# Seven of sixteen row blocks by a seven-product scheme, and one weight sum formed by transfers

## The chip, the cores and the metric

The kernel runs on one core of a Trainium2 chip. The metric is the device time of one execution in microseconds (us); the time before is the median of three runs. A profile holds one execution. Its engines are PE (the matrix engine), DVE (the vector engine), ACT (the scalar engine), POOL (the general-purpose engine) and SP, which here only issues transfers. ACT and POOL can issue transfers too; each engine issues its own in order.

## The reference

Four layers work on 256 frames of 1024 channels. Each adds a token mixer (retention, convolution, stick-breaking attention, retention) and then a feed-forward part:

```python
def squared_relu_mlp(xn, w1, w2):
    h = jax.nn.relu(xn @ w1)
    return (h * h) @ w2

for i in range(DEPTH):                      # 4
    ...
    x = x + m
    x = x + squared_relu_mlp(rms_norm(x, norm_ffn[i]), ffn_w1[i], ffn_w2[i])
return rms_norm(x, final_norm)
```

All data is float32; `w1` is 1024x4096 and `w2` is 4096x1024. The change concerns `(h * h) @ w2`, in the text the *down product*: 256 rows by 4096 by 1024, once per layer.

## The kernel before

**Split operands.** A float32 product is made of three matmuls on rounded operands: each operand is a high part (a cast, `wh` for a weight) plus a low part (source minus high part, `wl`), and high·high, high·low and low·high are added. Casts of weights are done by ACT (L362), the subtractions by DVE (L369), a tile of 128x1024 at a time. There are 5 buffers for `wh` and 5 for `wl`, so ACT's cast of a new tile waits until PE has read the last matmul of the tile five back.

**Weights.** They come from `in_w` in chunks of 1 MB (`raw`, 3 buffers) by SP in a fixed order (L348). A chunk holds two tiles of 128x1024.

**The down product** (`down`, L684). The 4096 rows of `w2` are 16 units `kb` of 256 rows; one unit is one 1 MB chunk. `C[t, c]` are four 128x512 accumulators in PSUM (`acc`) for two row halves t and two column halves c. `triple` (matmul at L689) issues the three matmuls of one product and keeps them in program order, so that PE runs the units in the order of the table `MIXED` and then `REST`.

A *plain* unit takes 8 products, thus 24 matmuls, two casts and two subtractions of 1024 columns. A *fast* unit (`FAST`) views its weights as four 128x512 blocks b11, b21, b12, b22 and the activations as four blocks of 128x128 columns, and takes 7 products by Strassen's scheme in Winograd's form, thus 21 matmuls. It needs the weight sums t1 = b11+b12, t3 = b12+b22, t2 = t1+b22 and t4 = t2+b21, added on DVE in `fast_unit` at L385, cast at L392 and subtracted at L393 in pieces of 512 columns. Its activation sums (`s1` to `s4`) are formed when the unit's activations leave the first product (L644 to L653) and rest in `big` or `z` tiles until used. Four of the seven products go to accumulators of their own in PSUM (`mis`: p1, p5, p7, p6), shared by all fast units; the others go straight to `C`.

After `MIXED` the four are combined into `C` through `big` tiles on ACT and DVE (L728 to L735, L759, L760), while PE goes on with the units of `REST`: first column half 0 of all of them, then column half 1, with one load of each chunk. When a column half is done the results are scaled, added to the residual, and handed to the next layer's mixer (L774, L787). The last layer ends in the final norm.

**Order.** Within an engine, instructions stand in an order that a scheduler sets at build time from estimated durations, unless `keep_in_program_order` binds them; at run time every engine runs its own list in order and waits for semaphores. Of temporary 128x512 tiles (`t`) there are 10. Constants, the retention decays among them, sit in one tile `cst`.

## Time and profile before

| what | value |
|---|---|
| median of three runs | 1329.37 us (1328.36 to 1329.39) |
| the profiled execution's own time | 1329.23 us |
| its span on the core | 1327.5 us |
| PE busy | 1316.6 us (99%), 7703 matmuls |
| DVE busy | 1063.9 us (80%) |
| ACT busy | 860.1 us (65%) |
| POOL busy | 154.1 us (12%) |
| `MIXED` of the first layer in the trace | 293.56 to about 356 us |

The span runs from the first to the last instruction of the profiled execution; the run's time is 1.7 us longer. "Busy" counts instructions in execution. On PE each matmul is drawn longer than its distance to the next, since they overlap. In a timeline a row gives start, duration, engine, line, operation, output and inputs, and in brackets how long the engine sat idle before it and what released it.

### The profile page before, as it was taken

The page shows a single profiled execution, that of the slowest core. Times are in us where ns is not written, and L with a number is a line of the kernel's source. Part 1 is how long each engine was busy: PE and PEld are TensorE (multiplying, and loading weights), DVE is VectorE, ACT ScalarE, POOL GpSimd, SP SyncE. Part 2 cuts the span into 40 slices and gives each one's busy share as a digit, 9 for nine tenths or more (in the row PEclk, how much of TensorE's full clock was granted, in tenths as well). Part 3 has the DMA queues.
Part 4 walks back from the last instruction along what each step waited for, and adds up shares of the span by engine and source line. Part 5 has one row for each costly group of instructions (what it writes and reads, how often), then busy time and mean ns, then how long its engine had stood idle before and what let it go on. Part 6 is the DMA issues. An engine that isn't in the chain of part 4 may idle for free.

```text
span 1327.5 us, 20237 instructions
## 1 busy us (share of the span) xinstructions
PE 1316.6 (99%) x7703; PEld 1133.6 (85%) x7703; DVE 1063.9 (80%) x1805; ACT 860.1 (65%) x1407; POOL 154.1 (12%) x169
## 2 busy tenths in 40 slices
PE   9999999999999999999999999999999999999998
PEld 8988888888899898888888898888888888888886
DVE  7987877779778688798788588798798776798985
ACT  7555546886566478766668678866675555567663
POOL 3554411000009110000000010000020000100000
PEclk9999999999999999999999999999999999999999
DMA  8666655545765655545453355555454554555552
GB/s 312 211 218 223 227 206 191 190 159 201 277 240 152 202 182 193 188 161 220 158 189 130 127 193 189 190 190 210 169 193 171 189 180 160 206 202 191 177 192 94
DMA packets 46049, 253.95 MB, mean 191 GB/s; under 512 B 5376, under 2 KB 10112, under 8 KB 18560
## 3 DMA queue, kind: packets, MB, share of 16 engines
q1 hardware_dynamic: 43360, 245.32, 52.4%
q0 software_dynamic: 1728, 4.72, 0.9%
q10 hardware_dynamic: 864, 2.62, 0.6%
q8 instruction: 60, 0.98, 0.3%
q14 instruction: 37, 0.30, 0.1%
HBM read 245.99 MB, written 6.65 MB: 190 GB/s over the span
## 4 chain that ended last, share of the span: by engine, by line
PE 96%; DVE 2%; ACT 1%; DMA 0%; issue 0%
PE acc L577 22%; PE acc L689 19%; PE acc L573 11%; PE acc L1107 6%; PE acc L1109 6%; PE acc L1108 6%; PE mis L689 3%; PE acc L557 3%; PE acc L558 3%; PE acc L559 3%; PE mis L577 2%; PE acc L1275 1%; PE mis L573 1%; PE acc L1408 1%; DVE wl L393 1%; DVE t L385 1%
## 5 line engine op out<-in xcount | busy, mean ns | idle before, releaser
L369 DVE TENSOR_TENSOR wl<-raw,wh 128x1024 fp32r<-128x1024 f32 (+1 forms) x420 | 512.5, 1231 | 122.1 <-ACT wh L362 119.1
L362 ACT CAST wh<-raw 128x1024 fp32r<-128x1024 f32 (+1 forms) x420 | 433.2, 1041 | 232.4 <-PE acc L689 68.6
L577 PE MATMUL acc<-z,wh 128*128 128x512 f32 x1152 | 399.4, 393 | 0.0
L573 PE MATMUL acc<-z,wl 128*128 128x256 f32 x1152 | 317.6, 280 | 0.0
L689 PE MATMUL acc<-wh,big 128*128 128x512 f32 x800 | 255.9, 391 | 0.0
L577 PEld LDWEIGHTS acc<-z,wh 128*128 128x128 f32 x1152 | 214.2, 187 | 47.1
L573 PEld LDWEIGHTS acc<-z,wl 128*128 128x128 f32 x1152 | 216.9, 189 | 2.4 <-DVE t L602 0.3
L689 PEld LDWEIGHTS acc<-wh,big 128*128 128x128 f32 x800 | 150.2, 188 | 30.7
L689 PE MATMUL acc<-wl,big 128*128 128x512 f32 x400 | 156.2, 390 | 0.5 <-DVE wl L369 0.5
L1107 PE MATMUL acc<-wh,z 128*128 128x512 f32 x352 | 138.6, 394 | 0.0
L1109 PE MATMUL acc<-wh,z 128*128 128x512 f32 x352 | 137.3, 390 | 0.0
L1108 PE MATMUL acc<-wl,z 128*128 128x512 f32 x352 | 137.2, 390 | 0.0
L601 ACT COPY t<-acc 128x256 f32<-128x256 f32 x154 | 53.1, 371 | 57.3 <-PE acc L577 55.4
L689 PEld LDWEIGHTS acc<-wl,big 128*128 128x128 f32 x400 | 75.1, 188 | 17.6 <-DVE wl L369 1.8
L1107 PEld LDWEIGHTS acc<-wh,z 128*128 128x128 f32 x352 | 66.1, 188 | 15.2 <-issue 2.2
L1109 PEld LDWEIGHTS acc<-wh,z 128*128 128x128 f32 x352 | 66.1, 188 | 14.8 <-issue 0.8
L1108 PEld LDWEIGHTS acc<-wl,z 128*128 128x128 f32 x352 | 66.1, 188 | 13.3
L602 DVE TENSOR_TENSOR t<-acc,t 128x256 f32<-128x256 f32 x154 | 59.7, 419 | 17.9 <-ACT t L601 16.0
L392 ACT CAST wh<-t 128x512 fp32r<-128x512 f32 x80 | 47.1, 619 | 35.2 <-DVE t L385 12.3
L557 PE MATMUL acc<-z,wh 128*128 128x256 f32 x224 | 63.7, 284 | 0.0
L492 POOL TENSOR_TENSOR t<-t,t 128x512 f32<-128x512 f32 x15 | 24.2, 1612 | 339.1 <-ACT t L487 308.7
L558 PE MATMUL acc<-z,wh 128*128 128x256 f32 x224 | 63.4, 283 | 0.0
(300 smaller groups left out, 2098.6 us busy)
## 6 DMA issues: line engine op xcount, KB each, us to landing
raw<-in_w SPq DMA_DIRECT2D x214, 1024.0 KB, 4.9
strip<-st POOLq DMA_DIRECT2D x36, 128.0 KB, 4.0
big<-strip SPq DMA_DIRECT2D x18, 256.0 KB, 5.9
big<-in_gn SPq DMA_DIRECT2D x16, 256.0 KB, 5.3
raw<-in_w SPq DMA_DIRECT2D x7, 512.0 KB, 7.4
raw<-hd SPq DMA_DIRECT2D x8, 263.0 KB, 5.2
raw<-hd SPq DMA_DIRECT2D x8, 131.5 KB, 3.6
wh<-in_w ACTq DMA_DIRECT2D x2, 512.0 KB, 6.3
```

What stands on the lines that cost most here:

```text
L362: nc.scalar.copy(hi[:, s], src[:, s])
L369: self.nc.vector.tensor_sub(lo[:, s], src[:, s], hi[:, s])
L557: nc.tensor.matmul(o, wh[:, kk, cs], ah, start=st, stop=False, **kw)
L558: nc.tensor.matmul(o, wh[:, kk, cs], al, start=False, stop=False, **kw)
L573: mm = nc.tensor.matmul(ps[m][:, :S], wl[:, kk, cs], a[:, :S], start=first and kk == 0, stop=False, **kw)
L577: nc.tensor.matmul(ps[m], wh[:, kk, cs], a, start=False, stop=last and kk == 3, **kw)
L601: nc.scalar.copy(o[:, s], ps[m][:, S:])
L602: nc.vector.tensor_add(o[:, s], ps[m][:, :S], o[:, s])
L689: mm = nc.tensor.matmul(o, l, r, start=start and n == 0, stop=stop and n == 2, skip_group_check=True)
L1107: nc.tensor.matmul(ps[t], zh[:, s], wh[:, kk], start=k == 0, stop=False, skip_group_check=True)
L1108: nc.tensor.matmul(ps[t], zh[:, s], wl[:, kk], start=False, stop=False, skip_group_check=True)
L1109: nc.tensor.matmul(ps[t], zl[:, s], wh[:, kk], start=False, stop=k == 7, skip_group_check=True)
```

## The change

It changes the down product and where some constants and activation sums are kept.

- `FAST` grows from five units to seven: 9 and 12 are added. `MIXED` begins with two plain units (0, 1) in place of one, has the fast units 9, 12 and 13, 14 next to each other, and ends with fast unit 15. `REST` shrinks from four units to three (8, 10, 11).
- The weight sum t3 = b12+b22 is no longer added on DVE. `sum_ahead` loads b12 into a `t` tile by SP and then adds b22 to it with an accumulating transfer that POOL issues (line numbers of the changed kernel: L385 and L386). Two are issued before the first unit, then one in each fast unit, two fast units ahead. The POOL ones keep their program order.
- t1 = b11+b12 is written over b12 in the `raw` tile (L415), so that t1 and b22 stand side by side and are cast (L399) and subtracted (L400) as one piece of 1024 columns. t3 and t2 share one weight tile, t4 has half of another. t2 and t4 are still DVE adds (L417, L419).
- `issue_after` places a fast unit's first cast, and its first add, behind an earlier subtraction in the build-time order.
- The activation sums of seven fast units need more room than those of five: `spare` takes `big` tiles for the first two fast units, a tile shared with the retention decays (tag "decay") for unit 9, and `z0` to `z7` for the rest. The decays therefore have a tile of their own and are loaded a second time for the last layer (4 transfers of 192 KB). The final norm's gain, which sat in `z6` and `z7`, is now loaded into `big` tiles after `MIXED`.

```diff
@@ -56,9 +56,9 @@
-FAST = (5, 6, 13, 14, 15)
-MIXED = (0, 5, 1, 2, 6, 3, 13, 4, 14, 7, 15, 8)
-REST = (9, 10, 11, 12)
+FAST = (5, 6, 9, 12, 13, 14, 15)
+MIXED = (0, 1, 5, 2, 6, 3, 9, 12, 4, 13, 14, 7, 15)
+REST = (8, 10, 11)
 OUT_ORDER = [(kb, p) for g in (0, 2) for kb in range(4) for p in (g, g + 1)]
@@ -108,6 +108,7 @@
 NUNIT = len(PLAN)
 UPC = 2
 NCHUNK = NUNIT // UPC
+DECAY = [PLAN.index(u) // UPC + n for u in (PLAN[DST * UPC], ("ret_w_in", 1, "b", 0, DK)) for n in range(RH)]
@@ -348,10 +349,14 @@
                     nc.sync.dma_start(self.rawt[:, a : a + h], self.w_d[n][:, a : a + h])
             for _ in range(min(2, len(self.later))):
                 self.later.pop(0)()
-            i = self.un // UPC - DST
-            if 0 <= i < RH:
-                n = CCOL["D"] + i * 384
-                self.tc.keep_in_program_order(nc.sync.dma_start(self.cst[:, n : n + 384], self.cst_d[:, n : n + 384]))
+            if self.un // UPC in DECAY:
+                i = DECAY.index(self.un // UPC) % RH
+                if i == 0:
+                    self.decay = self.cp.tile([P, RH * 384], F32, name=self.nm("decay"), tag="decay")
+                n = i * 384
+                self.tc.keep_in_program_order(
+                    nc.sync.dma_start(self.decay[:, n : n + 384], self.cst_d[:, CCOL["D"] + n : CCOL["D"] + n + 384])
+                )
         o = self.un % UPC
         src = self.rawt[:, o * 1024 : (o + 1) * 1024]
@@ -366,32 +371,54 @@
     def unit_lo(self, u):
         hi, lo, src, cuts = u
         for s in cuts:
-            self.nc.vector.tensor_sub(lo[:, s], src[:, s], hi[:, s])
+            self.lo_ins = self.nc.vector.tensor_sub(lo[:, s], src[:, s], hi[:, s]).ins
         return hi, lo
+    def sum_ahead(self, l):
+        nc = self.nc
+        m = len(self.ahead)
+        if m < len(FAST):
+            kb = [k for k in MIXED if k in FAST][m]
+            d = self.w_d[PLAN.index(("ffn_w2", l, "a", kb, 0)) // UPC]
+            t = self.tmp()
+            nc.sync.dma_start(t, d[:, 1024:1536])
+            self.tc.keep_in_program_order(nc.gpsimd.dma_start(t, d[:, 1536:2048], accum_op=ALU.add))
+            self.ahead[kb] = t
+
+
     def fast_unit(self, name, l, kb):
         nc = self.nc
-        ah, al = self.unit((name, l, "a", kb, 0))
+        out = []
+
+        def parts(*ts):
+            h, g = (self.wp.tile([P, 1024], F32R, name=self.nm(t), tag=t) for t in ("wh", "wl"))
+            a = 0
+            for t in ts:
+                c = slice(a, a + t.shape[1])
+                nc.scalar.copy(h[:, c], t)
+                self.lo_ins = nc.vector.tensor_sub(g[:, c], t, h[:, c]).ins
+                a = c.stop
+            out.extend((h[:, c : c + 512], g[:, c : c + 512]) for c in range(0, a, 512))
+
+        with self.tc.issue_after(self.lo_ins):
+            hi, lo = self.unit((name, l, "a", kb, 0))
+        out = [(hi[:, c : c + 512], lo[:, c : c + 512]) for c in (0, 512)]
         o = self.un % UPC * 1024
         assert PLAN[self.un] == (name, l, "a", kb, 512) and o
         self.un += 1
-        b11, b21, b12, b22 = (self.rawt[:, n * 512 : (n + 1) * 512] for n in range(4))
-        t1, t2, t3, t4 = (self.tmp() for _ in range(4))
-        out = [(ah[:, :512], al[:, :512]), (ah[:, 512:], al[:, 512:])]
-        h = None
-        for n, (dst, x, y) in enumerate(((None, b22, None), (t1, b11, b12), (t3, b12, b22), (t2, t1, b22), (t4, t2, b21))):
-            if dst is not None:
-                nc.vector.tensor_add(dst, x, y)
-            else:
-                dst = x
-            if n % 2 == 0:
-                h = self.wp.tile([P, 1024], F32R, name=self.nm("wh"), tag="wh")
-                g = self.wp.tile([P, 1024], F32R, name=self.nm("wl"), tag="wl")
-            c = slice(n % 2 * 512, (n % 2 + 1) * 512)
-            nc.scalar.copy(h[:, c], dst)
-            nc.vector.tensor_sub(g[:, c], dst, h[:, c])
-            out.append((h[:, c], g[:, c]))
+        b11, b21, t1, b22 = (self.rawt[:, i * 512 : (i + 1) * 512] for i in range(4))
+        t3 = self.ahead[kb]
+        self.sum_ahead(l)
+        t2, t4 = (self.tmp() for _ in range(2))
+        with self.tc.issue_after(self.lo_ins):
+            nc.vector.tensor_add(t1, b11, t1)
+        parts(self.rawt[:, 1024:2048])
+        nc.vector.tensor_add(t2, t1, b22)
+        parts(t3, t2)
+        nc.vector.tensor_add(t4, t2, b21)
+        parts(t4)
+        out[2], out[3] = out[3], out[2]
         return out
@@ -623,7 +650,16 @@
     def ffn(self, i, nxt):
         nc = self.nc
         last = nxt is None
-        h, rb, fast = [], [], {}
+        h, rb, fast, room = [], [], {}, []
+
+        def spare(n):
+            if n < 4:
+                return self.bigt(F32R)
+            if n < 6:
+                if n == 4:
+                    room.append(self.cp.tile([P, RH * 384], F32R, name=self.nm("room"), tag="decay"))
+                return room[0][:, (n - 4) * 512 : (n - 3) * 512]
+            return self.zp.tile([P, 512], F32R, name=self.nm("z"), tag=f"z{n - 6}")
         def act(ps):
@@ -644,11 +680,7 @@
                 nc.vector.tensor_sub(v3(x[:, :S], 2, P), v3(s[:, :S], 2, P), v3(s, 2, S)[:, :, P:])
                 nc.vector.tensor_sub(s2, s[:, :P], s1)
                 nc.vector.tensor_sub(s4, s[:, S : S + P], s2)
-                n = 2 * FAST.index(p) - 4
-                hi, lo = (
-                    self.bigt(F32R) if n < 0 else self.zp.tile([P, 512], F32R, name=self.nm("z"), tag=f"z{n + o}")
-                    for o in range(2)
-                )
+                hi, lo = (spare(2 * FAST.index(p) + o) for o in range(2))
                 nc.scalar.copy(hi, x)
                 nc.vector.tensor_sub(lo, x, hi)
@@ -698,6 +730,9 @@
             return [tuple(v3(x, 2, 512)[:, kk] for x in w) for kk in range(2)]
         C = {}
+        self.ahead = {}
+        for _ in range(2):
+            self.sum_ahead(i)
         for kb in MIXED:
             if kb not in FAST:
                 for c in range(2):
@@ -734,6 +769,7 @@
         nc.vector.tensor_add(uq, u, e5)
         nc.vector.tensor_add(C[1, 1], C[1, 1], uq)
+        hook(C, "gain")
         if i == 0:
             self.strip_t = []
...
@@ -844,6 +878,10 @@
                 ))
         def hook(C, at):
+            if at == "gain":
+                for c in range(2):
+                    gain.append(self.bigt())
+                    nc.sync.dma_start(gain[c], self.fin_d[:, c * 512 : (c + 1) * 512])
             if at:
                 return
```

In the changed kernel the plain subtraction is at L374, the cast at L367 and the load of a chunk at L349. Over the program PE issues 6756 rows where it issued 6780, DVE 1822 for 1782, ACT 1364 for 1352, SP 314 for 282 and POOL 202 for 174. Three places of the first layer follow.

**DVE inside `MIXED`.** Before, a fast unit (13, its chunk is `raw_3625`), with the two subtractions of the plain unit 3 (`raw_3591`) in between:

```order
L385 TENSOR_TENSOR t_771_3631<-raw_3625 128x512
L385 TENSOR_TENSOR t_773_3633<-raw_3625 128x512
L385 TENSOR_TENSOR t_772_3632<-t_771_3631,raw_3625 128x512
L385 TENSOR_TENSOR t_774_3634<-t_772_3632,raw_3625 128x512
L369 TENSOR_TENSOR wl_3594<-raw_3591,wh_3593 128x1024
L369 TENSOR_TENSOR wl_3610<-raw_3591,wh_3609 128x1024
L369 TENSOR_TENSOR wl_3628<-raw_3625,wh_3627 128x1024
L393 TENSOR_TENSOR wl_3636<-raw_3625,wh_3635 128x512
L393 TENSOR_TENSOR wl_3636<-t_771_3631,wh_3635 128x512
L393 TENSOR_TENSOR wl_3644<-t_773_3633,wh_3643 128x512
L393 TENSOR_TENSOR wl_3644<-t_772_3632,wh_3643 128x512
```

After, the fast unit 9 (`raw_3558`, its t3 is `t_721`) and the begin of unit 12:

```order
L374 TENSOR_TENSOR wl_3561<-raw_3558,wh_3560 128x1024
L415 TENSOR_TENSOR raw_3558<-raw_3558 128x512
L417 TENSOR_TENSOR t_760_3567<-raw_3558 128x512
L419 TENSOR_TENSOR t_761_3568<-t_760_3567,raw_3558 128x512
L400 TENSOR_TENSOR wl_3571<-raw_3558,wh_3570 128x1024
L400 TENSOR_TENSOR wl_3576<-t_721_3394,wh_3575 128x512
L400 TENSOR_TENSOR wl_3576<-t_760_3567,wh_3575 128x512
L400 TENSOR_TENSOR wl_3583<-t_761_3568,wh_3582 128x512
L374 TENSOR_TENSOR wl_3610<-raw_3607,wh_3609 128x1024
L415 TENSOR_TENSOR raw_3607<-raw_3607 128x512
L417 TENSOR_TENSOR t_772_3616<-raw_3607 128x512
L419 TENSOR_TENSOR t_773_3617<-t_772_3616,raw_3607 128x512
```

One add of 512 columns is gone; the two subtractions of [t1] and [b22] have become one of 1024; unit 12's follow with no plain unit between.

**SP at the head of the stage.** Before (L348 is the load of a chunk):

```order
L348 DMA raw_3387<-in_w 128x2048
L348 DMA raw_3421<-in_w 128x2048
L348 DMA raw_3455<-in_w 128x2048
L348 DMA raw_3506<-in_w 128x2048
L348 DMA raw_3540<-in_w 128x2048
L348 DMA raw_3591<-in_w 128x2048
```

After (L349 is the load of a chunk; L385 is here the load of b12 into a `t` tile, not the add that had this number before). `raw_3441` is unit 2, `raw_3475` the fast unit 6, `t_702` the sum of the first fast unit 5:

```order
L349 DMA raw_3441<-in_w 128x2048
L349 DMA raw_3475<-in_w 128x2048
L385 DMA t_702_3310<-in_w 128x512
L385 DMA t_703_3313<-in_w 128x512
L385 DMA t_721_3394<-in_w 128x512
L385 DMA t_742_3481<-in_w 128x512
L349 DMA raw_3524<-in_w 128x2048
L349 DMA raw_3558<-in_w 128x2048
L385 DMA t_759_3564<-in_w 128x512
L349 DMA raw_3607<-in_w 128x2048
L349 DMA raw_3656<-in_w 128x2048
L385 DMA t_771_3613<-in_w 128x512
```

Four loads for sums now stand between the chunk of unit 6 and the next one; the POOL transfers that add b22 to them (L386) follow each of them in time.

**ACT at the first fast unit.** Before (unit 5, `t_708` is t1, `t_709` t3, `t_710` t2, `t_711` t4; then unit 1):

```order
L412 CAST big_3274<-t_688_3272 128x256
L412 CAST big_3277<-t_688_3272 128x256
L392 CAST wh_3342<-t_708_3338 128x512
L392 CAST wh_3350<-t_710_3340 128x512
L392 CAST wh_3350<-t_709_3339 128x512
L652 CAST z_3284<-t_691_3280 128x512
L392 CAST wh_3358<-t_711_3341 128x512
L362 CAST wh_3389<-raw_3387 128x1024
L362 CAST wh_3405<-raw_3387 128x1024
```

After (unit 5 is `raw_3388`, `t_722` is t2 and `t_702` the transferred t3; `raw_3441` is unit 2):

```order
L439 CAST big_3290<-t_694_3288 128x256
L439 CAST big_3293<-t_694_3288 128x256
L399 CAST wh_3400<-raw_3388 128x1024
L399 CAST wh_3405<-t_722_3397 128x512
L399 CAST wh_3405<-t_702_3310 128x512
L399 CAST wh_3412<-t_723_3398 128x512
L684 CAST z_3300<-t_697_3296 128x512
L367 CAST wh_3443<-raw_3441 128x1024
L367 CAST wh_3459<-raw_3441 128x1024
```

The cast of the transferred t3 stands third of unit 5's four; the cast of t4, one activation cast and all of unit 2 stand behind it.

More of the change, by code (lines that the diff above doesn't have):

```diff
@@ L268, in __init__ @@
         self.prm = self.cp.tile([P, NPCOL - NP0], F32, name="prm", tag="prm")
-        self.cst = self.cp.tile([P, NCCOL], F32, name="cst", tag="cst")
+        self.cst = self.cp.tile([P, CCOL["D"]], F32, name="cst", tag="cst")
         self.first = [self.raw.tile([P, RAWW], F32, name=f"raw{n}", tag="raw") for n in range(3)]
@@ L831, in final @@
         self.table("sqrt_and_others")
-        gain = [self.zp.tile([P, 512], F32, name=self.nm("gain"), tag=f"z{6 + c}") for c in range(2)]
-        for c in range(2):
-            nc.sync.dma_start(gain[c], self.fin_d[:, c * 512 : (c + 1) * 512])
+        gain = []
         rows = []
@@ L1005, in retention @@
                     out=a[t], in0=ps[:, c0:c1], scalar=ck[:, t * 4 + h : t * 4 + h + 1],
-                    in1=self.c("D", c1 - c0, h * 384 + c0), op0=ALU.mult, op1=ALU.mult,
+                    in1=self.decay[:, h * 384 + c0 : h * 384 + c1], op0=ALU.mult, op1=ALU.mult,
                 )
```

## The prediction

> **What bounds the kernel now.** I read the page first: span, busy shares, granted clock, the chain that ended last.
>
> ```profile
> span 1327.5 us, 20237 instructions
> PE 1316.6 (99%) x7703; PEld 1133.6 (85%) x7703; DVE 1063.9 (80%) x1805; ACT 860.1 (65%) x1407; POOL 154.1 (12%) x169
> PEclk9999999999999999999999999999999999999999
> PE 96%; DVE 2%; ACT 1%; DMA 0%; issue 0%
> ```
>
> PE is busy all through, its clock is full in all slices, and the chain is PE for 96%. So time is won by giving PE fewer matmuls, as long as DVE (80%) and ACT keep ahead of it. Second the chain in order of time, in the first layer's down product (start, length, what):
>
> ```profile
> 303.34 1.15 DVE wl L369
> 304.53 10.96 PE acc L689 x47
> ...
> 319.57 6.12 PE acc L689 x27
> ```
>
> 27 matmuls in 6.12 us: 0.2267 us each. A plain unit of 24 is 5.44 us, a fast one of 21 is 4.76 us. The chain also shows DVE just before 304.53: PE waits there once. Third, the waits of PE, and its timeline at that place (start, duration, instruction, matmuls):
>
> ```profile
> PE acc L689 <- DVE wl L369: 0.5, 3, 0.2
> ```
>
> ```profile
> 303.21 0.39 PE L689 MATMUL acc<-wh,big 128*128 128x512 f32 x1
> 303.43 0.46 PE L689 MATMUL acc<-wl,big 128*128 128x512 f32 x1
> 303.73 0.63 PE L689 MATMUL acc<-wh,big 128*128 128x512 f32 x2
> 304.53 0.50 PE L689 MATMUL acc<-wl,big 128*128 128x512 f32 x1 [0.17 <-DVE wl L369]
> 304.87 0.62 PE L689 MATMUL acc<-wh,big 128*128 128x512 f32 x2
> ```
>
> From 303.21 to 304.87 lie five starts, 1.66 us where five intervals are 1.13: 0.53 us lost, at three places in the program. It is the first plain unit behind the first fast one, which in the old order comes when only one plain unit has gone before. Last, the engines by stretches of the stage (PE, PEld, DVE, ACT, POOL, granted clock, DMA share, GB/s):
>
> ```profile
> 282.00:293.00 11.00, 11.00 (x66) 9.69 (x65) 9.54 (x20) 8.92 (x17) 0.00 (x0) 1.00 0.54 188
> 293.00:304.00 11.00, 11.00 (x53) 8.97 (x51) 9.32 (x21) 7.99 (x14) 0.00 (x0) 1.00 0.11 36
> 304.00:315.00 11.00, 10.83 (x48) 8.68 (x47) 11.00 (x15) 6.00 (x9) 0.00 (x0) 1.00 0.75 266
> ```
>
> DVE is the next bound: 11.00 of 11 us at 304 to 315. ACT has room, POOL is idle, and transfers take little of the first 11 us.
>
> **The change part by part.**
>
> *Matmuls.* Two more units per layer go from 24 to 21: 4 x 2 x 3 = 24 matmuls x 0.2267 = **-5.44 us**. The listed order of PE is 24 shorter as well, so that this part isn't done is excluded.
>
> *DVE and ACT per unit.* The rows (DVE, then ACT):
>
> ```profile
> 318.40 2.35 DVE L369 TENSOR_TENSOR wl<-raw,wh 128x1024 fp32r<-128x1024 f32 x2
> ...
> 321.27 1.89 DVE L393 TENSOR_TENSOR wl<-t,wh 128x512 fp32r<-128x512 f32 x3
> ...
> 315.57 1.05 ACT L362 CAST wh<-raw 128x1024 fp32r<-128x1024 f32 x1 [1.60 <-PE acc L689]
> ...
> 320.13 1.66 ACT L392 CAST wh<-t 128x512 fp32r<-128x512 f32 x3
> ```
>
> In a row a DVE piece of 1024 columns costs 1.15 and one of 512 costs 0.6; a cast 1.0 and 0.52. A fast unit before was one of 1024, five subtractions and four adds of 512: 1.15 + 9 x 0.6 = 6.55 us of DVE. After, it is two of 1024, three subtractions and three adds: 2.3 + 3.6 = 5.9. ACT: 1.0 + 5 x 0.52 = 3.6 before, 2.0 + 3 x 0.52 = 3.56 after. DVE for the new `MIXED`: 7 x 5.9 + 6 x 2.3 = 55 us, against 7 x 4.76 + 6 x 5.44 = 66 us of PE. On the whole DVE keeps up; what must be looked at is pairs of fast units (9, 12 and 13, 14), where DVE needs 11.8 us and PE 9.5.
>
> Count such a pair from the moment PE enters its first unit, with DVE up to date. The weight tile that the second unit's cast needs comes free about then; from the rows, ACT starts 0.25 us behind the last matmul's slot:
>
> ```profile
> 315.10 0.39 PE L689 MATMUL acc<-wh,big 128*128 128x512 f32 x1
> 315.33 0.39 PE L689 MATMUL mis<-wh,big 128*128 128x512 f32 x1
> ```
>
> The cast is done at 1.3, the subtraction at 2.5, three adds at 4.3, the next subtraction of 1024 at 5.45. PE wants that one as the second matmul of the third product: 4.76 + 2 x 0.68 + 0.23 = 6.35. Margin 0.9 us, so 0. If DVE were not up to date (the cover gone), see the second rival.
>
> *Start of the stage.* Two plain units come first: 48 x 0.2267 = 10.9 us in place of 5.4 before the first fast unit. PE enters it at 293.6 + 10.9 = 304.5. DVE's work on it (5.9 us) and on the last activations stands in 293 to 304 as before, where 9.32 of 11 us are used, with the same next plain unit 5.44 us later than before. The 0.53 goes away in three layers: **-1.6 us**; between 0 and -1.6, taken at the far end since the stall was one of 0.53 and the room gained is ten times that.
>
> *The transferred sum.* No accumulating transfer is in the trace. Its neighbours are POOL's transfers of 128 KB at L898, SP's of 256 KB behind weights at L1047, and 256 KB alone at L834 (min/median/max in each):
>
> ```profile
> L898 POOL DMA_DIRECT2D strip<-st x36: 539/580/712, 65.4 to 172.9; - x36
> ...
> DMA to landing us min/median/max: 2.0/4.0/6.3
> ...
> L1047 SPq DMA_DIRECT2D big<-in_gn x16: 395/424/707, 102.9 to 1097.6; - x16
> ...
> DMA to landing us min/median/max: 5.0/5.3/6.8
> ...
> L834 SPq DMA_DIRECT2D gain<-in_fin x2: 328/328/328, 1234.8 to 1235.5; - x2
> ...
> DMA to landing us min/median/max: 2.7/2.8/2.9
> ...
> raw<-in_w SPq DMA_DIRECT2D x214, 1024.0 KB, 4.9
> ```
>
> From 256 KB (2.8) to 1 MB (4.9) a transfer grows by 2.1 us in 768 KB, 0.35 per 128 KB. The accumulating one is of 256 KB: 4.0 + 0.35 = 4.35; if the target's 256 KB are read too, 0.7 more. Bounds: 2.8 below (the row of 256 KB alone), 6.3 + 1.05 = 7.35 above (the slowest strip, grown alike). I take the middle of 4.35 and 5.05, **4.7**, since the strips are the only POOL transfers here.
>
> When must the first one be there? SP issues it behind the chunk of unit 6, whose buffer comes free with the second subtraction of unit 1, about 293.6; the load of b12 goes out at 294.0 and lands 5.3 later, 299.3; POOL's transfer starts at 299.4. It is late if it lands after 305.5, because behind its cast (0.52) ACT has t4's cast (0.52), an activation cast (0.52) and unit 2's first (1.0), and then DVE's subtraction (1.2) must reach PE at 304.5 + 4.76 + 0.23 = 309.5. So it has 6.1 us and needs 4.7: 1.4 spare, cost **0**. The upper bound 7.35 would cost 1.25 in each of four layers. Queued behind ACT's wait are those casts, behind DVE's the subtractions of unit 2, and PE waits for these. Every later sum is issued two fast units ahead, more than 10 us (4.76 + 5.44) before use, and needs 5.3 + 4.7 at its two steps; its last cast is some units on, so 0. SP's four loads stand ahead of the next chunk, which waits anyway for a buffer that DVE frees at about 302.
>
> [...]
>
> *Two more fast activations.* Their sums (DVE, DVE, DVE, ACT), made during the first product:
>
> ```profile
> 284.85 0.42 DVE L644 TENSOR_TENSOR t<-t 128x256 f32<-128x256 f32 x1
> ...
> 285.63 0.29 DVE L645 TENSOR_TENSOR t<-t,t 128x128 f32<-128x128 f32 x1
> ...
> 290.34 0.69 DVE L653 TENSOR_TENSOR z<-t,z 128x512 fp32r<-128x512 f32 x1
> ...
> 289.07 0.62 ACT L652 CAST z<-t 128x512 fp32r<-128x512 f32 x1
> ```
>
> With two at 0.29 this is 1.7 us of DVE and 0.6 of ACT for each unit. In 282 to 293, where units 13 and 14 do it, DVE is at 9.54 of 11 and PE at 11.00; so nothing. Without that cover it would be the 1.7.
>
> *End of the stage.* `REST` has three units: the last column half is 4 x 0.68 = 2.72 us shorter, and ACT's turn comes that much earlier:
>
> ```profile
> 373.44 0.61 ACT L487 ACTIVATE t<-x 128x512 f32<-128x512 f32 x1
> 373.96 1.03 ACT L362 CAST wh<-raw 128x1024 fp32r<-128x1024 f32 x1
> 376.27 0.69 ACT L774 ACTIVATE t<-acc,r 128x512 f32<-128x512 f32 x1 [1.28 <-PE acc L689]
> 377.44 0.60 PE L787 MATMUL mis<-cst,t 128*128 128x128 f32 x4
> ```
>
> The accumulator is there at 376.27 - 2.72 = 373.55, ACT at 373.96, as the cast now stands elsewhere: 0.41 late. From L774's end (376.96) to PE's use (377.44) there are 0.48. I allow 0.1 in three layers, **+0.3** (bounds 0 and 1.2).
>
> *Reloaded decays, gain, more traffic.* 28 sums move 0.5 MB each in stretches at a DMA share of 0.11 to 0.75: 0.
>
> Sum: -5.44 - 1.6 + 0.3 = **-6.7 us**, against the profiled execution's 1329.23: 1322.5. That execution lies 0.14 below the median, so **1322.6**. Its own range adds the stall not regained (+1.6), the end (+0.9), and 1.3 below for a first sum or an end with no cost: 1321.3 to 1325.1.
>
> **The rivals.**
>
> *The first sum is late by little.* A POOL transfer as slow as the slowest strip: 1.25 x 4 = 5.0, **1327.6**. For it: the strips spread from 2.0 to 6.3. Against it: POOL and the DMA queues are nearly idle then (share 0.11).
>
> *DVE bounds the pairs.* If DVE enters a pair behind by one subtraction of 1024 and one of 512, 1.75 us, the margin of 0.9 turns into 0.85 lost: x 2 x 4 = 6.8, **1329.4**, as before; at one of the two pairs alone, 1326.0. For it: DVE at 11.00 of 11. Against: plain unit 3 (2.3 us of DVE in 5.44 of PE) stands before one pair, unit 4 before the other.
>
> *Slower: accumulating takes twice a transfer.* If a sum of 256 KB takes 2 x 4.7 = 9.4 us, PE stops behind the first fast unit for 3.3 us in each layer, 13.2 in all: **1335.8**. It decides from (1332.0 - 1322.6) / 4 + 6.1 = 8.45 us on. For it: nothing in the trace bounds that operation from above. Against: twice as much is moved at a rate that shows 0.35 per 128 KB.
>
> **How the numbers follow.** Forecast 0.62, late by little 0.16, pairs 0.11, slower 0.11. What a measurement of this kernel can tell from no change is about 0.2%, 2.7 us: faster is below 1326.7, slower above 1332.0. Faster: 0.62, the quicker part of the first rival, 0.06, and one pair alone, 0.04: 0.72. Same: the rest of these two, 0.10 + 0.07: 0.17. Slower: 0.11. The range takes the forecast's lower end and reaches to the first rival's upper part: 1320.9 to 1329.2.
>
> **What would show it.** Right: 24 fewer matmuls at L721 and a span near 1320.8; PE's waits without the row of 0.5 us on DVE `wl`; POOL's L386 with a landing of 4 to 6 us, and ACT's cast of t3 without a wait for it. Wrong: PE waiting for `wl` of the plain subtraction right behind the first fast unit (late sum; the landing tells which rival), or for L400 inside units 12 and 14 (DVE), or idle time at the turn near the stage's end.

## The result

| | median | range |
|---|---|---|
| before | 1329.38 us (8 runs) | 1328.24 to 1331.75 |
| changed | 1323.36 us (8 runs) | 1322.93 to 1327.73 |

The ratio is 0.9954, with a 95% interval of 0.9944 to 0.9964: 6.0 us less, where 6.8 had been predicted (1322.6). The changed kernel's profiled execution took 1323.18 us, its span is 1321.4 us, 6.1 less than before. Its page:

```profile
span 1321.4 us, 20394 instructions
PE 1311.8 (99%) x7679; PEld 1129.8 (86%) x7679; DVE 1090.9 (83%) x1845; ACT 869.7 (66%) x1419; POOL 185.3 (14%) x197
PEclk9999999999999999999999999999999999999999
PE 97%; DVE 1%; ACT 1%; POOL 0%; issue 0%; POOLq 0%; ACTq 0%
t<-in_w SPq DMA_DIRECT2D x28, 256.0 KB, 5.5
t<-in_w POOLq DMA_DIRECT2D x28, 256.0 KB, 6.0
```

PE has 24 matmuls fewer (7703 to 7679), its mean granted clock is 1.000, and the 28 sums stand in the last two rows with their landing. All waits of PE that the trace lists:

```profile
PE mis L301 <- POOL t L273: 1.3, 1, 1.3
PE mis L464 <- POOL t L527: 0.7, 1, 0.7
PE acc L1313 <- issue: 0.4, 1, 0.4
PE mis L1331 <- issue: 0.2, 1, 0.2
```

The row of 0.5 us at the plain subtraction is gone and nothing of the down product is in its place. In the chain in order of time, the head of the first layer's stage, which is to be set beside the one shown of before:

```profile
293.50 11.03 PE acc L721 x48
304.54 0.68 PE mis L721 x3
305.22 1.36 PE acc L721 x6
306.58 2.04 PE mis L721 x9
308.62 6.12 PE acc L721 x27
```

48 plain matmuls, then a fast unit and the next plain one without a gap. From here on I use a stage's length: from the start of the first to the start of the last matmul of a layer's down product (first and last start of the groups of L689 or L721). Each kernel's four layers, and the time outside them:

| kernel | stage 1 | 2 | 3 | 4 | sum | outside |
|---|---|---|---|---|---|---|
| before | 85.5 | 85.5 | 85.5 | 84.4 | 340.8 | 986.6 |
| changed | 83.6 | 83.6 | 83.6 | 83.1 | 333.8 | 987.6 |

The stages gave 7.0 us, which is the predicted -5.44 - 1.6 with nothing for the end. Of that, 1.0 was lost outside: the stretch between the third and the fourth stage, where the wait on L527 stands, grew by 1.2 (288.2 us before, 289.5 after), and the others together are 0.3 shorter. One of the eleven executions of a kernel below (eight fast units in pairs) took 4566.91 us, the others 1327.09 to 1331.68; its ratio is that of the others.

### The profile page after: what moved, and what is told of

The parts are those of the page before. It is cut to its first block, busy times and chain, and to the rows that moved or that the text cites. A ratio compares the mean times of both kernels' runs of the same rounds, so it can differ in the third digit from the quotient of the medians.

```text
span 1321.4 us, 20394 instructions
## 1 busy us (share of the span) xinstructions
PE 1311.8 (99%) x7679; PEld 1129.8 (86%) x7679; DVE 1090.9 (83%) x1845; ACT 869.7 (66%) x1419; POOL 185.3 (14%) x197
## 4 chain that ended last, share of the span: by engine, by line
PE 97%; DVE 1%; ACT 1%; POOL 0%; issue 0%; POOLq 0%; ACTq 0%
PE acc L604 22%; PE acc L721 19%; PE acc L600 11%; PE acc L1145 6%; PE acc L1147 6%; PE acc L1146 6%; PE mis L721 6%; PE acc L584 3%; PE acc L585 3%; PE acc L586 3%; PE mis L604 2%; PE acc L1313 1%; PE mis L600 1%; PE acc L1446 1%; PE mis L464 1%; PE mis L1034 1%
## 5 line engine op out<-in xcount | busy, mean ns | idle before, releaser
L374 DVE TENSOR_TENSOR wl<-raw,wh 128x1024 fp32r<-128x1024 f32 (+1 forms) x412 | 505.0, 1236 | 110.3 <-ACT wh L367 107.4
L367 ACT CAST wh<-raw 128x1024 fp32r<-128x1024 f32 (+1 forms) x412 | 423.9, 1041 | 198.3 <-PE acc L1147 67.2
L721 PE MATMUL acc<-wh,big 128*128 128x512 f32 x704 | 228.7, 391 | 0.0
L721 PEld LDWEIGHTS acc<-wh,big 128*128 128x128 f32 x704 | 132.2, 188 | 27.1
L721 PE MATMUL acc<-wl,big 128*128 128x512 f32 x352 | 137.0, 389 | 0.0
L386 POOL DMA_DIRECT2D t<-in_w x28 | 24.9, 1089 | 458.5 <-DMA t<-in_w 327.5
L721 PEld LDWEIGHTS acc<-wl,big 128*128 128x128 f32 x352 | 66.1, 188 | 13.4
L519 POOL TENSOR_TENSOR t<-t,t 128x512 f32<-128x512 f32 x15 | 24.2, 1613 | 340.8 <-ACT t L514 310.5
L399 ACT CAST wh<-raw 128x1024 fp32r<-128x1024 f32 x28 | 29.5, 1052 | 58.5 <-DVE raw L415 56.2
L584 PE MATMUL acc<-z,wh 128*128 128x256 f32 x224 | 63.7, 284 | 0.0
```

Source lines behind the costliest of these rows:

```text
L367: nc.scalar.copy(hi[:, s], src[:, s])
L374: self.lo_ins = self.nc.vector.tensor_sub(lo[:, s], src[:, s], hi[:, s]).ins
L584: nc.tensor.matmul(o, wh[:, kk, cs], ah, start=st, stop=False, **kw)
L721: mm = nc.tensor.matmul(o, l, r, start=start and n == 0, stop=stop and n == 2, skip_group_check=True)
```

## The experiments

In the table at the end of this section the kernels are set side by side. Ratios are to the kernel before, which ran beside them on the same chip; "+x us" compares stage lengths with those of the changed kernel.

### The order alone

The kernel before, with five fast units and its own sums; only the second plain unit comes earlier:

```diff
-MIXED = (0, 5, 1, 2, 6, 3, 13, 4, 14, 7, 15, 8)
+MIXED = (0, 1, 5, 2, 6, 3, 13, 4, 14, 7, 15, 8)
```

> The kernel before with one edit: two plain units (0, 1) before the first fast one. Five fast units, sums on DVE as before. Theory: the 0.53 us stall behind the first fast unit goes in the three layers that had it, so -1.6 us, span about 1325.9, and the row of PE waiting for the plain subtraction is gone; the down product lasts 84.9 us from its first to its last matmul in place of 85.4. Rival (the stall comes with the first fast unit wherever it stands): no change, the row stays.

Ratio 0.9987 (0.9977 to 0.9997). The stages are 84.9, 84.9, 84.9 and 84.4 us: 0.6 less in each of the three layers that had the stall, nothing in the fourth, 1.7 in all, and PE's wait for the plain subtraction is gone. The term of -1.6 is right.

### The sum on DVE again

```diff
-        t3 = self.ahead[kb]
-        self.sum_ahead(l)
-        t2, t4 = (self.tmp() for _ in range(2))
+        t2, t3, t4 = (self.tmp() for _ in range(3))
         with self.tc.issue_after(self.lo_ins):
-            nc.vector.tensor_add(t1, b11, t1)
+            nc.vector.tensor_add(t3, t1, b22)
+        nc.vector.tensor_add(t1, b11, t1)
...
```

> The changed kernel, but t3 = b12+b22 is a DVE add again (t1 still written in place, no transferred sums). DVE then needs 2.3 + 7 x 0.6 = 6.5 us per fast unit in place of 5.9. Theory (matmuls set the time, DVE has 0.9 us to spare in a pair): one pair keeps 0.9 - 0.6 = 0.3 us, but a cycle of one plain and two fast units needs 2.3 + 13.0 = 15.3 us of DVE against 5.44 + 9.5 = 14.97 of PE, so DVE falls behind 0.3 us a cycle: 0 to 1.5 us lost per layer, in all +0 to +6 against the changed kernel, taken as +2 (about 1325.4). Rival A (the transfers are what makes seven units pay): PE waits for DVE in each pair, +6 or more, no better than the kernel before. Rival B (the transfers buy nothing): the same time as the changed kernel, no wait of PE on DVE in the stage.

Ratio 1.0026 (1.0015 to 1.0036), slower than before the change: the outcome of rival A. The stages are 2.9, 2.8, 2.8 and 2.4 us longer than the changed kernel's. PE's waits in the stages:

```profile
PE acc L720 <- DVE acc L766: 4.2, 4, 1.2
PE acc L720 <- DVE wl L400: 2.9, 4, 0.7
```

The 0.7 is DVE's lag at unit 14, as counted (PE's second matmul of that product starts 1.12 us behind the first, 0.9 more than the interval). The larger one I had not counted: it is the add into C[1,1] at the end of the stage, which DVE's list here has behind the adds into C[0,0] and C[1,0]. So the run doesn't price the sum alone. A second one holds the subtractions of `REST`'s second half back, behind that add (here and below, remarks behind a `#` are not in the kernel):

```diff
-        nc.vector.tensor_add(C[1, 1], C[1, 1], uq)
+        c11 = nc.vector.tensor_add(C[1, 1], C[1, 1], uq).ins
 ...
+                with self.tc.issue_after(after):      # after = c11, column half 1 only
+                    w = self.unit_lo(u)
```

> Seven fast units with all sums on DVE, with the same edit at the end of the stage. In the run without it the stage was 3.0 us longer than in the changed kernel: 0.9 at unit 14 (PE waiting for L400), the rest at the end, at the add into C[1,1]. Theory: the end was the order's doing, the 0.9 is what the sum on DVE costs; stages of 84.4 us, +3.6 us in all against the changed kernel, about 1327, still below the kernel before. Rival (DVE's lag itself comes out at the end, in whatever order): stages of 86 us, no better than before.

Ratio 1.0001 (0.9991 to 1.0012). The wait for the add is gone, the one of 0.7 at L400 is there four times, and in two layers PE now waits up to 1.3 us for ACT at the turn to the next layer:

```profile
PE mis L824 <- ACT t L811: 2.1, 2, 1.3
```

Stages of 86.0, 86.5, 84.9 and 84.4. The fourth layer, which has no turn, is 1.3 us over the changed kernel and so is the third. In the third, 1.0 of it is the lag at unit 14 and the matmul behind it, and 0.3 is the same lag at unit 12, too short there to be listed as a wait (three matmuls start at 900.54, 900.95 and 901.29, 0.75 us where two intervals are 0.45). My theory held for that place and fell for the sum of the time: seven units with their sums on DVE, in both orders that were run, are not faster than five. Without the waits at the turn, with 84.9 in each of the first three layers, the stages would come to an estimated 339.1, which five units reach by their order alone (339.1). So in the orders that were run the transferred sum is what made the two more units pay. It is not shown that no order would do without it.

The edit itself, on the changed kernel:

> The changed kernel with that edit alone. Theory: nothing waits at the end of its stage, so no change, stages of 83.5 us. Rival: the edit itself gains or costs, which would then have to be taken off the two runs beside it.

Stages of 84.5, 83.6, 83.6 and 83.1, ratio 0.9947 (0.9930 to 0.9964): no gain, and 0.9 us more in one layer, where PE waits 0.8 us for ACT at the turn. So the edit brings some of that wait along; in the run before it isn't all DVE's lag.

### How much room the first sum has

In the changed kernel ACT waited for the first sum in each layer. POOL's four transfers and then ACT in the first layer (start, duration, in brackets the idle time before):

```profile
299.61 3.66 POOL L386 DMA_DIRECT2D t<-in_w  x4 [87.23 <-DMA t<-in_w]
```

```profile
304.57 1.14 ACT L399 CAST wh<-t 128x512 fp32r<-128x512 f32 x2 [4.80 <-DMA t<-in_w]
```

From POOL's start to the cast are 4.96 us, where 4.7 had been taken for the landing, and the cast starts 0.9 us before the latest moment that the prediction worked out (305.5). Two runs give the needed sum a later place among those that POOL issues together:

```diff
-            kb = [k for k in MIXED if k in FAST][m]
+            kb = (6, 5, 9, 12, 13, 14, 15)[m]         # third place: (6, 9, 5, ...), three sums at the start
```

> The changed kernel, but of the sums formed ahead that of unit 6 is issued first and that of unit 5 (needed first) second. In the changed kernel's trace ACT's cast of the first sum begins 0.2 us after, 0.4, 0.2 and 0.7 us before PE enters the first fast unit (layers 1 to 4); by the prediction's chain it may begin 1.1 us after. If a place further back costs about 1.9 us (four issued in a row land within 4.6 to 10.5), the sum is late by 1.0, 0.4, 0.6 and 0.1 us: +2.1 us in all, PE waiting for a plain subtraction behind the first fast unit. Rival (more slack than the chain says): no change, ACT's wait grows, PE's doesn't.

> As the run before, with the sum of unit 5 in third place (three sums issued ahead: 6, 9, 5). Theory: late by another 1.9 us in each layer, 2.9 + 2.3 + 2.5 + 2.0 = +9.7 us against the changed kernel, about 1333. Rival (slack of 4 us or more): no change.

Ratios 1.0076 (1.0063 to 1.0090) and 1.0149 (1.0135 to 1.0163): +16.8 and +26.8 us in the stages, not +2.1 and +9.7. The direction and the existence of an edge are as the theory has it, its two sizes are wrong. First, a place further back costs more than 1.9 us. In second place, with PE's first fast unit at 305.69 (304.38 in the changed kernel):

```profile
301.36 3.67 POOL L386 DMA_DIRECT2D t<-in_w  x4 [87.66 <-ACT wh L399]
```

```profile
310.62 1.14 ACT L399 CAST wh<-t 128x512 fp32r<-128x512 f32 x2 [7.63 <-DMA t<-in_w]
```

The cast comes 4.9 us after PE's entry instead of 0.2, so 4.7 us later. The four landings there take 6.1 to 9.7 us, with a median of 8.9; in the changed kernel's first layer they take 4.9 to 10.5, with a median of 9.6. So the changed kernel's own trace has no even steps of 1.9: the first is quick and the others are late.

What goes along with it stands in SP's list. In the changed kernel a chunk of 1 MB goes out 1.26 us behind POOL's first transfer, in this run 0.84 us (302.20):

```profile
300.87 9.06 SPq L349 DMA_DIRECT2D raw<-in_w  x2
```

In the first three layers of the ten kernels with transferred sums, the first sum issued took 4.0 to 4.9 us where the chunk followed by 1.2 us or more (21 places), and 5.1 to 8.1 where it followed within 1.0 (9 places, longer the closer it followed); in the fourth layers, with 2.4 us or more, it took 4.0 to 6.1. A sum alone on its way does the same in the changed kernel itself: 4.7 us for the one issued at 329.40, with a chunk 1.15 us behind it, and 7.3 for the one at 604.26, with a chunk 0.60 behind. No run moves the chunk alone, so that the chunk is the cause is argued and not shown.

Second, the wait of PE isn't the whole price. PE, and the windows around the wait (PE, PEld, DVE, ACT, POOL, granted clock, DMA share, GB/s):

```profile
308.19 0.39 PE L721 MATMUL mis<-wh,big 128*128 128x512 f32 x1
311.29 0.51 PE L721 MATMUL mis<-wh,big 128*128 128x512 f32 x1 [2.71 <-ACT wh L399]
312.02 0.80 PE L721 MATMUL mis<-wl,big 128*128 128x512 f32 x1 [0.22 <-DVE wl L400]
...
313.89 0.63 PE L721 MATMUL mis<-wh,big 128*128 128x512 f32 x1
314.32 0.63 PE L721 MATMUL acc<-wh,big 128*128 128x512 f32 x1
```

```profile
308.00:311.00 3.00, 0.58 (x3) 0.15 (x1) 0.00 (x0) 0.38 (x1) 0.00 (x0) 1.00 1.10 234
312.00:313.00 1.00, 0.98 (x2) 0.83 (x3) 0.83 (x2) 1.00 (x2) 0.00 (x0) 0.50 0.30 51
313.00:315.00 2.00, 2.00 (x6) 1.57 (x5) 2.00 (x2) 1.60 (x2) 0.00 (x0) 0.50 0.00 0
315.00:316.00 1.00, 1.00 (x5) 0.78 (x5) 1.00 (x2) 0.00 (x0) 0.00 (x0) 0.82 0.00 0
```

Behind the wait the granted clock is 0.50 for 3.4 us (in the third layer for 6.8), and a matmul starts every 0.43 us (313.89 to 314.32) in place of 0.2267. This layer's stage is 5.1 us longer (88.7 for 83.6): about 3.4 us of waits (308.19 to 312.02, less two intervals) and about 1.7 of slow matmuls. The wait also stands at another place than I wrote: at the product that uses t3 itself, not at the next unit's subtraction, because a sum that is 4.9 us late misses that as well.

The reverse: the first unit's t3 on DVE, which had been idle there, and the other six by transfer.

```diff
+        t3 = self.ahead.get(kb)
+        if t3 is None:
+            t3 = self.tmp()
+            with self.tc.issue_after(self.lo_ins):
+                nc.vector.tensor_add(t3, t1, b22)
...
```

> The changed kernel, but t3 of the first fast unit (5) alone is a DVE add; the other six units keep their transferred sums. In the changed kernel DVE sat idle 3.6 us and ACT 4.8 us there, waiting for that sum. Theory (the wait lies in slack that PE never sees): no change of the time, 1323.4 with stage lengths of 83.5 us, no wait of ACT on a transferred sum at the first fast unit. Rival (the late first sum does cost PE something, or feeds a lag that is carried on): stages shorter by 0.3 us or more.

Stages of 83.6, 83.6, 83.6 and 83.1, ratio 0.9948 (0.9935 to 0.9961): the changed kernel's, with no wait of ACT on a transferred sum. The 4.8 us that ACT stood there cost PE nothing.

### The microsecond outside the stages

```diff
-            nc.gpsimd.tensor_add(sq, sq, self.sq[:, S:])
+            nc.vector.tensor_add(sq, sq, self.sq[:, S:])
```

> The changed kernel, but the half-sum of the norm (L527) is added by DVE in place of POOL. In the changed kernel's trace PE waits 0.7 us for it in the last layer, behind a POOL add (L968) that lasted 4.8 us where the one of the kernel before lasted 0.75, and the stretch between the third and the fourth down product is 289.4 us long where it was 288.2. Theory (POOL's add is held by DVE's operations, and the norm's add stands behind it): the wait of PE on L527 goes and the stretch is 288.2 to 288.7, -0.7 to -1.2 us. Rival (the longer stretch has another cause): 289.4 stays.

The wait of 0.7 us is gone, the stages are the same, the stretch is 288.9 us, between the theory's 288.2 to 288.7 and the rival's 289.4; ratio 0.9946 (0.9932 to 0.9959). It says less than I hoped, since in this execution POOL's other adds there weren't long in the first place (the longest took 1.56 us). What settles more is that add in the other traces. POOL in the kernel before, and in the changed one:

```profile
959.70 0.75 POOL L930 TENSOR_TENSOR big<-t 128x256 f32<-128x256 f32 x1 [180.11 <-ACT t L921]
```

```profile
953.77 4.81 POOL L968 TENSOR_TENSOR big<-t 128x256 f32<-128x256 f32 x1 [56.81 <-ACT t L959]
958.54 1.35 POOL L527 TENSOR_TENSOR t<-t 128x256 f32<-128x256 f32 x1
```

```profile
957.89 0.75 DVE L629 TENSOR_TENSOR t<-acc,t 128x256 f32<-128x256 f32 x2
```

It lasts 0.75 us or 4.8. Where it is short, DVE's next operation is long, 1.24 us for 0.69, as in the kernel before:

```profile
959.76 1.24 DVE L492 TENSOR_TENSOR t<-t,t 128x512 f32<-128x512 f32 x1
```

The run with the order alone, which has no transfers, no new tiles and no sums ahead, has the long one and PE's wait of 0.7 us as well (min/median/max of the group in the stretch's first part):

```profile
L930 POOL TENSOR_TENSOR big<-t x5: 1004/1309/4811, 958.3 to 984.1; 128x256 f32<-128x256 f32 x5
```

The second run of eight units in pairs, below, has the short one, no wait there, and a stretch of 287.7. So the microsecond isn't the transfers' or the new tiles'. Over all fourteen traces the add is long in nine, with PE's wait of 0.7 us in each of them, and short in five, with DVE's next operation at 1.24 to 1.26 us. In all of them it starts while DVE is busy, 0.04 to 0.06 us ahead of DVE's next operation, so the moment of its start doesn't tell which of the two is the long one; what decides that is open. In the changed kernel's trace the long add ends at 958.58, 0.7 us after DVE, busy without a gap until then, comes to the first addition since the add's start of which one operand is in PSUM (957.89, the row of DVE above). That the one ends because of the other is not shown.

### Eight fast units

Eleven fits as an eighth fast unit if the last third of the tile that holds unit 9's activation sums is used too and there are 9 temporary tiles in place of 10.

```diff
+FAST = (5, 6, 9, 11, 12, 13, 14, 15)
+MIXED = (0, 1, 5, 2, 6, 9, 3, 11, 12, 4, 13, 14, 15)
+REST = (7, 8, 10)
```

> Eight fast units (11 added), REST = 7, 8, 10, in the order 0, 1, 5, 2, 6, 9, 3, 11, 12, 4, 13, 14, 15, so that three stand in a row at the end; 9 temporary tiles in place of 10. Twelve matmuls fewer: -2.72 us. A fast unit takes DVE 6.14 us by the changed kernel's trace, PE 4.76, and a pair had 0.68 us to spare: the third in a row is late by 1.38 - 0.68 = 0.7 us, and the first plain unit behind it by up to as much again, 2.8 to 5.6 us in four layers. Theory: 1323.4 - 2.7 + 2.8 to 5.6 = 1323.5 to 1326.3, PE waiting for L400 in unit 15. Rival (DVE's lead is larger than counted): 1320.7, no wait. Rival (a lag carried into the combination, as with all sums on DVE): slower than 1327.

Ratio 1.0096 (1.0082 to 1.0110), stages of 89.8, 89.7, 89.7 and 84.8. The third unit in a row is late by the 0.7 us that the arithmetic gave (the third row), and the sum over it is wrong again, for what was left out:

```profile
PE acc L721 <- DVE acc L770: 7.9, 4, 2.2
PE mis L721 <- ACT wh L399: 4.4, 3, 2.1
PE acc L721 <- DVE wl L400: 2.6, 4, 0.7
```

The add into C[1,1] comes last again, and the first sum is late: ACT's cast starts at 308.90, 8.1 us behind POOL's first issue (300.81). It is the pattern of above at its closest: SP's next chunk goes out 0.28 us behind POOL's first transfer, where the changed kernel had 1.26.

```profile
300.81 3.66 POOL L386 DMA_DIRECT2D t<-in_w  x4 [88.25 <-DVE wl L400]
```

```profile
301.09 0.33 SPq L349 DMA_DIRECT2D raw<-in_w  x1
```

The next one avoids both the triple and the late first sum, the latter by forming the first unit's t3 on DVE as above:

```diff
-MIXED = (0, 1, 5, 2, 6, 9, 3, 11, 12, 4, 13, 14, 15)
+MIXED = (0, 1, 5, 6, 2, 9, 11, 3, 12, 13, 4, 14, 15)
...
```

> Eight fast units as well, but in four pairs with a plain unit between (0, 1, 5, 6, 2, 9, 11, 3, 12, 13, 4, 14, 15), and the first unit's t3 by DVE, so that the first pair doesn't start late. A cycle of one plain and two fast units is 2.3 + 2 x 6.14 = 14.6 us of DVE against 14.97 of PE, each pair has 0.68 us. Theory: no wait of PE in the stage but at most one at its end, -2.72 us against the changed kernel: 1320.7, stages of 82.8 us. Rival (the sums' transfers or the weight chunks come too late with pairs from the start): PE waits for t3's cast, and with the lower granted clock behind each such wait some 4 us per layer are lost.

Ratio 1.0000 (0.9990 to 1.0009). `MIXED` runs without a wait, as the theory said. At the end of each stage PE waits for the add into C[1,1], 1.8 us in the first three layers and 0.7 in the fourth. In the first and the third it then runs at half clock for 3.4 us, in the second, after the same wait, it does not; the stages are 86.6, 85.5, 86.6 and 83.4. The expectation allowed one wait there and no slow matmuls. In the first layer:

```profile
367.78 0.39 PE L726 MATMUL acc<-wh,big 128*128 128x512 f32 x1
370.01 0.50 PE L726 MATMUL acc<-wh,big 128*128 128x512 f32 x1 [1.83 <-DVE acc L775]
```

```profile
371.00:372.00 1.00, 1.00 (x4) 0.81 (x3) 0.07 (x1) 0.00 (x0) 0.00 (x0) 0.50 1.04 402
```

With the subtractions of `REST`'s second half held back, as above:

> The kernel with eight fast units in pairs, and one more edit: the DVE subtractions of the second column half of REST are placed behind the add into C[1,1]. In the run without it MIXED took 65.4 us, the 8 x 4.76 + 5 x 5.44 = 65.3 of its matmuls alone, and PE waited 1.8 us at the end for the add into C[1,1], which DVE had in its list behind seven such subtractions and the adds into C[0,0] and C[1,0]; 11 matmuls then ran at half the granted clock. Theory: that order is the whole loss, so stages of 82.8 us (83.5 less 3 matmuls), -2.7 us against the changed kernel, about 1320.7, and no wait of PE on DVE. Rival (DVE is simply full, 60.6 of 65.3 us in MIXED, and something else comes late in its place): stages of 84 us or more, PE waiting for a plain subtraction of REST.

Ratio 0.9947 (0.9933 to 0.9962): stages of 84.3, 84.7, 83.3 and 82.4. The wait for the add is gone. The last layer is 0.7 us shorter than with seven units, three matmuls as counted. The first two wait at the turn, for the scaling of C[0,1] by ACT:

```profile
PE mis L833 <- ACT t L820: 2.0, 2, 1.3
```

A cast of the next layer stands before it in ACT's list, and a subtraction of the next layer before the adds into C[0,0] and C[1,0] in DVE's. Both behind:

```diff
+        if self.hold is not None:                       # the add into C[1,0]; next layer's first subtraction
+            after, self.hold = self.hold, None
+            with self.tc.issue_after(after):
+                return self.unit_lo(u)
...
+        behind = self.hold_hi if self.un == self.hold_un else None   # the scaling of C[0,1]; third cast
+        with self.tc.issue_after(behind) if behind is not None else nullcontext():
```

> The kernel with eight fast units in pairs and the subtractions of REST held back, with two more edits at the turn to the next layer: the adds into C[0,0] and C[1,0] come before the next layer's first subtraction on DVE, and ACT's cast of the next layer's third tile comes behind the scaling of C[0,1]. In the run without them PE waited 0.7 and 1.3 us there for that scaling, and the stages were 84.3, 84.7, 83.3 and 82.4 us. Theory: with MIXED at the speed of its matmuls and neither wait, 82.8, 82.8, 82.8 and 82.4 us: -2.7 us against the changed kernel, 1320.7 where that takes 1323.4, a ratio of 0.993 to the kernel before. Rival (with eight fast units DVE and ACT have no room left at the end, whatever the order): another wait takes the place, stages of 83.5 us or more, no gain over seven units.

1321.03 us (1318.46 to 1321.95), ratio 0.9923 (0.9909 to 0.9937): faster than both kernels. Stages of 83.1, 83.1, 83.1 and 82.4, no wait of PE inside them that the trace lists; three of them are 0.3 over the theory's. Of that, 0.2 stand at the turn, where PE goes on 0.05 us behind the end of ACT's scaling (374.90 behind 374.85), a wait too short to be listed. The range of the ratio lies below that of the changed kernel; since both are set against the kernel before in different sessions, the 2.1 us by which the stages are shorter (331.7 for 333.8) are the better measure of the step from seven to eight. In `MIXED` DVE has little left, 0.14 of 11 us in this stretch:

```profile
337.00:348.00 11.00, 11.00 (x51) 9.09 (x50) 10.86 (x14) 7.41 (x10) 1.13 (x3) 1.00 0.75 237
```

### Side by side

| kernel | ratio to before | sum of the four stages |
|---|---|---|
| before, 5 units | 1 | 340.8 |
| changed, 7 units | 0.9954 | 333.8 |
| order alone, 5 units | 0.9987 | 339.1 |
| 7, all sums on DVE | 1.0026 | 344.8 |
| 7, all sums on DVE, end reordered | 1.0001 | 341.8 |
| 7, end reordered | 0.9947 | 334.8 |
| 7, first sum on DVE | 0.9948 | 333.8 |
| 7, norm's add on DVE | 0.9946 | 333.8 |
| 7, first sum second | 1.0076 | 350.6 |
| 7, first sum third | 1.0149 | 360.6 |
| 8, a triple at the end | 1.0096 | 353.9 |
| 8, pairs | 1.0000 | 342.1 |
| 8, pairs, end reordered | 0.9947 | 334.7 |
| 8, pairs, end and turn reordered | 0.9923 | 331.7 |

## Why the prediction was right, point by point

- **The bound.** PE, before and after; a shorter list of matmuls became time one for one in the stages.
- **Matmuls, -5.44.** The fourth layer, which never had the stall, shows it alone: 84.4 to 83.1, 1.4 us for 6 x 0.2267 = 1.36.
- **The stall, -1.6.** Shown by itself by the order alone. The three other layers are 1.9 shorter: 1.36 and the 0.53.
- **DVE in pairs, margin 0.9.** It was 0.7. The step to mend is the 0.6 us taken for each of three adds. In the pair of units 9 and 12 (PE enters unit 9 at 324.77), DVE:

```profile
326.10 1.23 DVE L374 TENSOR_TENSOR wl<-raw,wh 128x1024 fp32r<-128x1024 f32 x1 [1.30 <-ACT wh L367]
327.24 0.69 DVE L415 TENSOR_TENSOR raw<-raw 128x512 f32<-128x512 f32 x1
327.96 0.69 DVE L417 TENSOR_TENSOR t<-raw 128x512 f32<-128x512 f32 x1
328.69 0.69 DVE L419 TENSOR_TENSOR t<-t,raw 128x512 f32<-128x512 f32 x1
329.30 1.22 DVE L400 TENSOR_TENSOR wl<-raw,wh 128x1024 fp32r<-128x1024 f32 x1
```

  t2 needs t1 and t4 needs t2, so these start 0.72 us apart, not 0.6; the subtraction behind t4, which doesn't need it, starts 0.61 us after it. A fast unit is 6.14 us of DVE (326.10 to the next unit's subtraction at 332.24), not 5.9. The subtraction's slot ends at 330.44 and PE uses it at 331.12.
- **The transferred sum at no cost.** The cost is right: taken as 4.7 us, measured 4.96 to the cast; 0.9 of the 1.4 us of room were left. (The prediction's own terms put the latest moment at 309.5 - 1.2 - 1.0 - 3 x 0.52 = 305.7, not 305.5.) But its sign, a cast of t3 for which ACT doesn't wait, did not show: ACT waited 4.8 us, at no cost. And in part it was luck. The prediction let SP's next chunk go out at about 302 and gave it no effect; it went out at 300.87, 1.26 us behind POOL's transfer, and first sums with less than 1.0 between the two took 5.1 to 8.1 us. The 4.7 fits the first of the four alone; the others took 9.4 to 10.5 in the first layer. Six of the seven uses a layer cost nothing even so, being issued two fast units ahead, though landings went up to 11.4 us:

```profile
L386 POOL DMA_DIRECT2D t<-in_w x28: 872/888/1702, 299.6 to 1270.1; - x28
...
DMA to landing us min/median/max: 4.0/6.0/11.4
```

- **The end, +0.3.** It was 0, inside the bounds given. ACT's scaling of C[0,1] starts at 374.57 and PE uses it at 375.32:

```profile
374.57 0.67 ACT L810 ACTIVATE t<-acc,r 128x512 f32<-128x512 f32 x1
```

  Between the end of the scaling and its use lie 0.08 us, and where PE has to wait it goes on 0.05 behind it (376.05 behind 376.00 in the second run of eight units in pairs), so some 0.03 are to spare. The first runs with an edited end (both of seven units, and eight in pairs) fell over that edge.
- **Outside the stages.** No term was given; +1.0 us. Matmul for matmul beside the kernel before, 0.95 us come in where PE waits for the norm's half-sum (959.95 and 960.08), behind the long add on POOL; the rest are small steps both ways. Predicted -6.7, plus 1.0, less the 0.3 not spent, is the span's -6.1 within rounding.
- **The rivals.** None came true. The two that the sum is late were priced as the wait alone. For 1.25 us that holds by these runs, where no wait of 1.05 to 1.7 us was followed by slow matmuls; for the slower rival's 3.3 us it doesn't, since each wait of 2.5 us and more was. Its break-even of 8.45 us is a wait of 2.35 us, between those where both occur and those that always were, so it may be too high. The rival that DVE bounds the pairs is what happens when one more add is left on DVE, but about half of it by way of the end of the stage (1.45 of 2.9 us in the first layer), which I had looked at for ACT and not for DVE.
- **The range.** Its lower end, 1320.9, lies 0.4 below the forecast's own 1321.3, and of the 1.3 us below the forecast only the 0.3 of the end could be gained, since the first sum was already taken at 0. Neither bears on the outcome.

## What to carry to other kernels

Where one engine bounds, a cut of its work is worth its full price only while every helper stays ahead at every place, so count the margin of the helper at the tightest place and not its share of the stage; here it was 0.7 us in a pair and some 0.03 at the turn. When a helper falls behind, look at the tail too, where its list holds work that is needed soon behind work that is needed late: without the edits of order there an eighth unit cost 8 us in the stages, with them it gave 2. And price a long wait of PE as the wait and the slow matmuls behind it: in these runs they followed all eight waits of 2.5 us and more, and three of the eight from 1.8 to 2.3 us. Where a transfer has little room, look at what large transfer goes out right behind it: in the first three layers here, first sums took 5.1 to 8.1 us with a chunk of 1 MB within 1.0 us behind them, and 4.0 to 4.9 with 1.2 us or more between.

## What the hardware showed that was not expected

- After a wait of PE the granted clock fell to 0.50 for 3.4 us, twice for 6.8. Behind the start, the traces have 26 waits of PE over 1 us: all eight of 2.5 us and more were followed by it, three of the eight from 1.8 to 2.3 us, and none of the ten from 1.05 to 1.7. One length can go both ways: of the waits of 1.8 us in the first run of eight units in pairs, those in the first and the third layer were followed by it and that in the second was not. The shortest wait that was followed by it is thus one of 1.8 us, the longest that was not is one of 2.2; what decides between them is not shown.
- Of transfers that POOL issues one behind the other, only the first was quick: in the first three layers of the changed kernel it took 4.6 to 4.9 us and the other three 9.4 to 11.4. The first took up to 8.1 us where SP's next 1 MB went out 0.3 us behind it.
- One POOL add of 128x256 took 0.75 us or 4.8 us, started at the same place among DVE's operations. Where it took 0.75, DVE's next operation took 1.24 in place of 0.69.
